# A decoder layer in split fp32 on one core: lo parts written over loaded tiles, and shorter pauses before the up projection

## The chip, the cores and the metric

The kernel runs on one core of a Trainium2 chip. The metric is the device time of one execution in microseconds. A core has TensorE (PE in the profile: matmuls and transposes), VectorE (DVE), ScalarE (ACT), GpSimd (POOL, nearly unused here) and SyncE (SP, which issues the DMA transfers in the order of its queue). "PEld" is the loading of weights into TensorE.

## The reference

One layer of a decoder over 2048 positions of 1024 channels, all in float32:

```python
h = rms_norm(x, mix_norm_g)
z = h @ w_in                                   # 1024 -> 2048
lru_x, lru_gate, conf_a, conf_b = split(z, 4)
y_lru = rg_lru(causal_dwconv(lru_x, ...), ...) * gelu(lru_gate)
c = silu(layer_norm(causal_dwconv(conf_a * sigmoid(conf_b), ...)))
x = x + concat([y_lru, c]) @ w_out

h, m = rms_norm(x, xa_norm_g), rms_norm(mem, mem_norm_g)
q, (k, v) = h @ w_q, split(m @ w_kv, 2)        # 256 memory tokens, 4 heads
p = softmax(q @ k.T * XA_HD ** -0.5)
x = x + (p @ v) @ w_o

h = rms_norm(x, ffn_norm_g)
g, u = split(h @ w_up, 2)                      # 1024 -> 2 x 3072
g = causal_dwconv(g, ffn_conv_w, ffn_conv_b)
x = x + (gelu(g) * u) @ w_down                 # 3072 -> 1024
return rms_norm(x, final_norm_g)
```

## The kernel before

**Split products.** A float32 matrix is split in two parts that TensorE multiplies at its rounded fp32 rate: `hi`, the value rounded (written by ScalarE as a copy), and `lo`, the value less `hi` (a subtraction by VectorE). A product of two such matrices is three matmuls, hi x hi, lo x hi and hi x lo (`mm3`). In the names of the profile `yh`/`yl`, `Xh`/`Xl`, `wh`/`wl` and `hidh`/`hidl` are such pairs. `parts(b)` makes the pair of a tile `b` in two new tiles; `split(src, hi, lo)` does it into tiles that were made before by `pair`.

**Seven products.** The large matrix products are done as 2 x 2 blocks with seven block products in place of eight, with sums and differences of blocks as operands (named S1 to S4 on one side and T1 to T4 on the other). `Quads` prepares the seven operands of three weight matrices ahead of time and keeps their pairs in DRAM: OUT_Q (w_out), A_Q (queries against memory keys), VO_Q (memory values times w_o; `VO` in the profile's DMA rows). `seven` runs the seven products of a stage of `attend(h)`, FIRST (w_out), SECOND (scores) and THIRD (probabilities times VO), for half `h` of the positions. In THIRD the last three products are P7, P2 and P3; `x_...` in the rows below are the residual tiles to which VectorE adds their banks, and `yh`/`yl` with `s<-pt,s` are the split of their left operand.

**The up projection.** `up(h, B)` goes over half `h` in blocks of columns; each block is seven products (`strassen_cols`) with weights loaded and split on the way (`raw`, `s`, `t`, `wh`, `wl`) and with operands `X` that are made once for a half (`HalfX.make`: loads `xn`, makes the differences `t`, and splits each into `Xh`, `Xl`). For half 0, `make` is called for the first four operands by a task `first_x` while the attention of half 1 still runs, with a pause between them; the three others are made by the first block itself. For half 1 the differences are made ahead by `X[1].kept` and come back as tiles `tx`; all seven operands of half 1 are made during the last block of half 0. `feed_forward` starts when both `first_x` and the last attention step are through. `T:xn`, that is `ps<-ident,xn` in the rows, are the transposes of normed tiles.

**The down projection.** `prepare_down` makes the seven operands of w_down and keeps their pairs in DRAM, paced along the up projection; `Down` loads hidden tiles, adds, splits and multiplies them.

**What sets the order.** The kernel is not written in the order in which it runs. Tasks (Python generators) record operations into a `Program`; `drive` advances the task that is due, by a clock of the matmuls recorded so far, and `yield n` asks to be called again n us later on that clock. When all is recorded, `schedule` gives each engine its own list: it simulates the engines with estimated lengths, picks the ready operation with the earliest due time, and gives tiles of a fixed set to those who ask, in the order in which they were recorded. The set has 85 slots of 128 x 512 floats, and 8 banks of PSUM. Every instruction bears the same line number, that of the place where lists are written out, so instructions are told apart by the names of their tiles.

Of the kernel before, what the change touches and what calls it, by code (L numbers as in the profile page):

```python
# [17 lines left out]
P = 128  # L18
# [81 lines left out]
class Ref:  # L100
    def __init__(self, buf, steps, dummy):
        self.buf, self.steps, self.dummy = buf, steps, dummy

    def __getitem__(self, i):
        return Ref(self.buf, self.steps + (lambda ap: ap[i],), self.dummy[i])

    def f32(self):
        return Ref(self.buf, self.steps + (lambda ap: ap.bitcast(F32),), self.dummy)
# [22 lines left out]
def resolve(a):  # L131
    return a.resolve() if isinstance(a, Ref) else a

# [13 lines left out]
class Program:  # L147
# [51 lines left out]
    def do(self, eng, name, out, *args, reads=(), writes=(), **kw):  # L199
        outs = [out] + ([kw["accum_out"]] if "accum_out" in kw else [])  # L200
        ins = [a for a in list(args) + list(kw.values()) if isinstance(a, Ref) and a not in outs]
        if eng == "PE":
            o = self.group or self.op("PE")
            n = ins[1].n if name == "matmul" else P
            if name == "matmul":
                rounded = ins[1].buf.dtype == F32R
                cost = (n + 32) / 2400.0 if rounded else n * 4 / 2400.0
            else:
                cost = 0.11
# [11 lines left out]
        o.calls.append((name, (out,) + args, kw))  # L221
        self.touch(
# [225 lines left out]
def hybrid_layer(  # L448
# [629 lines left out]
    class Quads:  # L1078
# [7 lines left out]
        def prepare(self, pace):  # L1086
            sub = ALU.subtract
            for i in range(KH):
# [37 lines left out]

    held = [0]

    def seven(order, L, W, add, amid):
        banks, left = {}, {}  # L1130
# [4 lines left out]
        for n, (p, bank, start, outs) in enumerate(order):  # L1135
# [4 lines left out]
            for i in range(KH):  # L1140
                lh, ll = parts(L.get(akey, i))
# [246 lines left out]
    class HalfX:  # L1388
# [40 lines left out]
        def make(self, key):  # L1429
            sub = ALU.subtract  # L1430
            if key in self.t:
# [13 lines left out]
            for b in src:  # L1445
                hi, lo = pair("X")
                split(b[:], hi, lo)
                self.B[key].append((hi, lo))

    def strassen_cols(c0, B, outs, used=None):  # L1450
# [11 lines left out]
        def product(bank, src, key, start):  # L1462
            X = B.get(key)
            wh, wl = pair("w", (P, KQ, P))
            split(src, wh, wl)
# [25 lines left out]
        product(c, s1[:], "T1", True)  # L1491
        yield 0
        s3 = comb(a11, a21, ALU.subtract)
        product(a, s3[:], "T3", False)
# [8 lines left out]
        product(c, s4[:], "B22", False)  # L1503
# [54 lines left out]
    def prepare_down():  # L1558
        yield attends[NH - 1]
        for c in range(NCK):  # L1560
            for i in range(KD):
                f = c * 2 * KD + i
                raw = []
                for r0 in (f * P, (f + KD) * P):
                    for half in range(2):
                        t = tmp("wd")
                        pr.dma(t[:], w_down[0, r0 : r0 + P, half * TT : (half + 1) * TT])
                        raw.append(t[:])
                b11, b12, b21, b22 = raw
                t1 = combine("t", b12, b11, ALU.subtract)  # L1570
                t2 = combine("t", b22, t1[:], ALU.subtract)
                t3 = combine("t", b22, b12, ALU.subtract)
                t4 = combine("t", b21, t2[:], ALU.subtract)
                for key, src in (("B11", b11), ("B21", b21), ("T2", t2[:]), ("T1", t1[:]), ("T3", t3[:]), ("T4", t4[:]), ("B22", b22)):
                    hi, lo = pair("w")
                    split(src, hi, lo)
# [5 lines left out]
    class Down:  # L1582
# [34 lines left out]
        def gather(self, c, n):  # L1617
# [192 lines left out]
```

## Time and profile before

| | us |
|---|---|
| median of 3 runs | 2493.47 |
| lowest and highest run | 2490.45, 2495.44 |
| the profiled execution | 2495.1 |
| its span, first to last instruction | 2493.3 |
| TensorE busy | 2421.8 |
| VectorE busy | 1921.3 |
| ScalarE busy | 1290.6 |

The mean granted clock of TensorE in the profiled execution is 0.988 of full speed. The times of a span are counted from its start. A row of a timeline gives the start, the length, the engine, the operation with the tiles it writes and reads, its size and the number of like instructions, and in brackets the idle time of the engine before it with what ended it. A row of the view by stages gives, for each engine, the busy time and the number of instructions, then the granted clock, the busy share of the DMA engines, and GB/s.

### The profile page before, as it was taken

Reading aid. Unit: us, or ns where it says so; the run is one execution under the profiler, and the core shown is the slowest. Engines: PE = TensorE matmul, PEld = TensorE weight load, DVE = VectorE, ACT = ScalarE, POOL = GpSimd, SP = SyncE. Lnnn points to the kernel's source line nnn. Section 1 sums busy time; section 2 is a strip of 40 time slices with the busy share of each in tenths; the row PEclk is TensorE's granted clock in tenths of the full one; section 3 lists DMA queues with packets and bytes.
Section 4 is the critical chain, followed back from the end, with each engine's and each line's share of the span. In section 5 each row is a group of like instructions: output and inputs, shape, how many; then the busy total and the mean of one; then the engine's idle time right before and its main releaser. Section 6 shows DMA issues by size and latency. Waiting matters only on the chain.

```text
span 2493.3 us, 32519 instructions
## 1 busy us (share of the span) xinstructions
PE 2421.8 (97%) x10788; PEld 1988.5 (80%) x10788; DVE 1921.3 (77%) x3187; ACT 1290.6 (52%) x2256; POOL 0.7 (0%) x6
## 2 busy tenths in 40 slices
PE   6999999999998999999999999999999999999998
PEld 5788868877767888878888887788888888888886
DVE  4579968999988645779888887987876775667665
ACT  8426668266977655775545455654443431233222
POOL 0000000000000000000000000000000000000000
PEclk8999999999999999999999999999999999999999
DMA  6987678797786966586654546644422288769774
GB/s 221 376 296 228 228 237 302 248 349 243 241 300 224 372 221 228 167 278 241 226 204 155 182 162 194 235 166 163 169 76 85 93 293 269 249 224 368 257 251 157
DMA packets 339839, 572.07 MB, mean 229 GB/s; under 512 B 32925, under 2 KB 106653, under 8 KB 339671
## 3 DMA queue, kind: packets, MB, share of 16 engines
q1 hardware_dynamic: 339670, 570.00, 67.0%
q8 instruction: 85, 1.39, 0.2%
q14 instruction: 84, 0.68, 0.1%
HBM read 385.32 MB, written 184.55 MB: 229 GB/s over the span
## 4 chain that ended last, share of the span: by engine, by line
PE 87%; DVE 5%; DMA 4%; ACT 3%; issue 1%; SPq 0%; DVEq 0%; ACTq 0%
PE ps L420 87%; ACT prob L420 1%; DVE yl L420 1%; DMA raw<-in_w_out_dram 1%; DVE t L420 1%; DMA VO<-VO 0%; DMA x<-in_x_dram 0%; DMA yf<-yf 0%; DVE s L420 0%; DVE prob L420 0%; DVE xc L420 0%; DVE gate L420 0%; ACT L420 0%; DVE Xl L420 0%; ACT x L420 0%
## 5 line engine op out<-in xcount | busy, mean ns | idle before, releaser
L420 PE MATMUL ps<-Xh,wl 128*128 128x512 f32 x1344 | 523.9, 390 | 2.5 <-DVE wl L420 2.5
L420 PE MATMUL ps<-Xh,wh 128*128 128x512 f32 x1344 | 524.3, 390 | 1.6 <-ACT wh L420 1.6
L420 PE MATMUL ps<-Xl,wh 128*128 128x512 f32 x1344 | 523.4, 389 | 0.0
L420 PEld LDWEIGHTS ps<-Xh,wl 128*128 128x128 f32 x1344 | 252.6, 188 | 57.1 <-DVE wl L420 4.7
L420 PEld LDWEIGHTS ps<-Xh,wh 128*128 128x128 f32 x1344 | 252.7, 188 | 55.3 <-ACT wh L420 2.9
L420 PEld LDWEIGHTS ps<-Xl,wh 128*128 128x128 f32 x1344 | 252.7, 188 | 52.1
L420 PE MATMUL ps<-wh,yh 128*128 128x512 f32 x672 | 268.9, 400 | 7.0 <-ACT pt L420 3.7
L420 PE MATMUL ps<-wh,yl 128*128 128x512 f32 x672 | 265.0, 394 | 4.9 <-DVE yl L420 4.9
L420 PE MATMUL ps<-wl,yh 128*128 128x512 f32 x672 | 264.5, 394 | 0.1
L420 PE MATMUL ps<-wh,hidh 128*128 128x512 f32 x672 | 261.4, 389 | 0.0
L420 PE MATMUL ps<-wl,hidh 128*128 128x512 f32 x672 | 261.4, 389 | 0.0
L420 PE MATMUL ps<-wh,hidl 128*128 128x512 f32 x672 | 261.4, 389 | 0.0
L420 DVE TENSOR_TENSOR acc<-acc,ps 128x512 f32<-128x512 f32 x192 | 129.5, 685 | 150.3 <-PE ps L420 149.9
L420 PE MATMUL ps<-xh,wh 128*128 128x512 f32 x512 | 201.8, 394 | 0.9 <-DMA wh<-w_in 0.8
L420 PE MATMUL ps<-xh,wl 128*128 128x512 f32 x512 | 199.5, 390 | 2.3 <-DVE wl L420 1.7
L420 PE MATMUL ps<-xl,wh 128*128 128x512 f32 x512 | 199.3, 389 | 0.0
L420 ACT ACTIVATE wh<-s 128x512 fp32r<-128x512 f32 x192 | 119.8, 629 | 136.5 <-DVE s L420 99.9
L420 PEld LDWEIGHTS ps<-wh,yh 128*128 128x128 f32 x672 | 128.0, 191 | 36.9 <-ACT pt L420 4.6
L420 PEld LDWEIGHTS ps<-wh,yl 128*128 128x128 f32 x672 | 127.9, 190 | 34.1 <-DVE yl L420 7.1
L420 DVE TENSOR_TENSOR wl<-s,wh 128x512 fp32r<-128x512 f32 x192 | 131.2, 688 | 27.3 <-ACT wh L420 25.4
L420 ACT ACTIVATE u<-ps 128x512 f32<-128x512 f32 x144 | 85.9, 597 | 126.5 <-PE ps L420 125.4
L420 PEld LDWEIGHTS ps<-wl,yh 128*128 128x128 f32 x672 | 128.2, 191 | 27.6 <-issue 0.8
(200 smaller groups left out, 4113.0 us busy)
## 6 DMA issues: line engine op xcount, KB each, us to landing
raw<-in_w_up_dram SPq DMA_DIRECT2D x96, 512.0 KB
wh<-w_down SPq DMA_DIRECT2D x164, 256.0 KB
wl<-w_down SPq DMA_DIRECT2D x164, 256.0 KB
hid<-cv SPq DMA_DIRECT2D x48, 512.0 KB
h<-hid SPq DMA_DIRECT2D x96, 256.0 KB
w_down<-wh SPq DMA_DIRECT2D x84, 256.0 KB
w_down<-wl SPq DMA_DIRECT2D x84, 256.0 KB
x<-in_x_dram SPq DMA_DIRECT2D x64, 256.0 KB
```

Of the source, the lines that this page charges most:

```text
L420: getattr(e, name)(*[resolve(a) for a in args], **{k: resolve(a) for k, a in kw.items()})
```

## The change

Two things are changed. First, `split_over(b)` makes the pair of a tile whose last use is this split: `hi` goes into a new tile, and `lo` is written over `b` itself, if `b` was loaded by DMA and no engine has written it since; else `lo` gets a new tile as before. It stands in `Quads.prepare`, in `seven` for the last use of a block, in `HalfX.make` (for all operands of half 1, and for the differences and the last block of half 0), in `strassen_cols`, in `prepare_down` and in `Down.gather`. The test on loaded tiles leaves 116 tiles: 36 in `Quads.prepare` (b11, b21, b22 of four steps of three matrices), 4 (the last block) of half 0's operands, all 28 of half 1's, 36 in `prepare_down`, and 12 in `Down` (A22 of half 0). The sums and differences that VectorE makes in the kernel get a new tile for `lo` as before. Second, `first_x` pauses 5 us on the recorder's clock after each of its four operands, where it paused 20. No operation is added or taken away.

```diff
@@ class Buf
-        self.ops, self.heads = [], []
+        self.ops, self.heads, self.loaded = [], [], True
@@ class Ref
+    def r(self):
+        return Ref(self.buf, self.steps + (lambda ap: ap.bitcast(F32R),), self.dummy, True)
...
+class Over:
+    def __init__(self, buf):
+        self.buf, self.dtype = buf, F32R
+
+    def __getitem__(self, i):
+        return self.buf[i].r()
@@ Program.do
+        for r in outs:
+            if not r.rounded:
+                r.buf.loaded = False
@@
+    def split_over(b, name):
+        hi, lo = rnd(name + "h", b.shape), Over(b) if b.loaded else rnd(name + "l", b.shape)
+        ACT(hi[:], b[:], AF.Copy)
+        V("tensor_tensor", lo[:], b[:], hi[:].f32(), op=ALU.subtract)
+        return hi, lo
@@ Quads.prepare
-                    for j, b in enumerate(parts(t)):
+                    for j, b in enumerate(split_over(t, "y")):
@@ seven
-                lh, ll = parts(L.get(akey, i))
+                lh, ll = split_over(L.get(akey, i), "y") if n in spent else parts(L.get(akey, i))
@@ HalfX.make
             for b in src:
-                hi, lo = pair("X")
-                split(b[:], hi, lo)
+                if self.h or key[0] == "T" or key == "B22":
+                    hi, lo = split_over(b, "X")
+                else:
+                    hi, lo = pair("X")
+                    split(b[:], hi, lo)
@@ prepare_down
-                    hi, lo = pair("w")
-                    split(src, hi, lo)
+                    hi, lo = split_over(src, "w")
@@ Down.gather
-                hi, lo = pair("hid")
-                split(src[:], hi, lo)
+                if akey in ("S1", "S3", "S4") or (akey == "A22" and not self.h):
+                    hi, lo = split_over(src, "hid")
+                else:
+                    hi, lo = pair("hid")
+                    split(src[:], hi, lo)
@@ first_x
         for key in UP_ORDER[:EARLY]:
             X[0].make(key)
-            yield 20
+            yield 5
```

Both move instructions, since the schedule is worked out anew from the tiles asked for and the order of recording. Three places are shown, each before and after.

TensorE, the end of the attention of half 1. The rows are the last products of THIRD (`wh`, `wl` are VO's pairs), the transposes of normed tiles, and the first products of the up projection (`Xh`, `Xl`). Before:

```order
L420 MATMUL ps<-wh,yh 128x512
L420 MATMUL ps<-wl,yh 128x512
L420 MATMUL ps<-wh,yl 128x512
L420 MATMUL ps<-ident,xn 128x128 x16
L420 MATMUL ps<-Xh,wh 128x512
L420 MATMUL ps<-Xl,wh 128x512
L420 MATMUL ps<-Xh,wl 128x512
L420 MATMUL ps<-Xh,wh 128x512
```

Changed:

```order
L436 MATMUL ps<-wh,yh 128x512
L436 MATMUL ps<-wl,yh 128x512
L436 MATMUL ps<-wh,yl 128x512
L436 MATMUL ps<-Xh,wh 128x512
L436 MATMUL ps<-Xl,wh 128x512
L436 MATMUL ps<-Xh,wl 128x512
L436 MATMUL ps<-Xh,wh 128x512
L436 MATMUL ps<-Xl,wh 128x512
```

In the changed order 144 up matmuls (six products) follow directly; then eight transposes stand, and the others in groups between later products.

VectorE, during P2 and P3 of the same stage. `x_...` are residual adds of P7 and P2 (the tile numbers differ between the kernels), `t<-xn` starts and `t<-xn,t` continues the differences for `X`, `yl<-s,yh` splits P3's operand. Before:

```order
L420 TENSOR_TENSOR x_7923<-x_7923,ps 128x512
L420 TENSOR_TENSOR x_7925<-x_7925,ps 128x512
L420 TENSOR_TENSOR t<-xn 128x512
L420 TENSOR_TENSOR x_7927<-x_7927,ps 128x512
L420 TENSOR_TENSOR x_7931<-x_7931,ps 128x512
L420 TENSOR_TENSOR t<-xn 128x512 x3
L420 TENSOR_TENSOR t<-xn,t 128x512 x6
L420 TENSOR_TENSOR x_8186<-x_8186,ps 128x512
L420 TENSOR_TENSOR t<-xn,t 128x512
L420 TENSOR_TENSOR Xl<-t,Xh 128x512
```

Changed:

```order
L436 TENSOR_TENSOR x_7887<-x_7887,ps 128x512
L436 TENSOR_TENSOR t<-xn 128x512 x2
L436 TENSOR_TENSOR yl<-s,yh 128x512
L436 TENSOR_TENSOR t<-xn,t 128x512
L436 TENSOR_TENSOR x_7889<-x_7889,ps 128x512
L436 TENSOR_TENSOR t<-xn,t 128x512 x2
L436 TENSOR_TENSOR s<-pt,s 128x512
L436 TENSOR_TENSOR t<-xn,t 128x512
L436 TENSOR_TENSOR x_7895<-x_7895,ps 128x512
L436 TENSOR_TENSOR yl<-s,yh 128x512
L436 TENSOR_TENSOR Xl<-t,Xh 128x512 x2
```

The differences for `X` have moved ahead of P2's adds and among the splits of P3's operand, which stood before them.

VectorE, the last block of half 0 of the up projection. `gb` and `up` take a bank out of PSUM, `cv` is the convolution over 1024 positions, `s` the weights' sums, `wl` their lo parts, `Xl` (in the changed kernel `xn`, the loaded tile itself) the lo parts of half 1's operands. Before:

```order
L420 TENSOR_TENSOR gb<-u,ps 128x512
L420 TENSOR_TENSOR Xl<-xn,Xh 128x512
L420 COPY gtail<-gb 128x2
L420 SCALAR_TENSOR_TENSOR cv<-gb,v_110,cv 128x1024
L420 TENSOR_TENSOR s<-raw 128x512
L420 TENSOR_TENSOR wl<-t,wh 128x512
L420 TENSOR_TENSOR s<-s,raw 128x512
L420 TENSOR_TENSOR up<-u,ps 128x512
L420 SCALAR_TENSOR_TENSOR cv<-gb,v_110,cv 128x1024
L420 TENSOR_TENSOR wl<-s,wh 128x512 x2
```

Changed:

```order
L436 TENSOR_TENSOR xn<-xn,Xh 128x512 x3
L436 TENSOR_TENSOR s<-raw 128x512
L436 TENSOR_TENSOR gb<-u,ps 128x512
L436 COPY gtail<-gb 128x2
L436 TENSOR_TENSOR s<-s,raw 128x512
L436 SCALAR_TENSOR_TENSOR cv<-gb,v_110,cv 128x1024
L436 TENSOR_TENSOR wl<-s,wh 128x512
L436 SCALAR_TENSOR_TENSOR cv<-gb,v_110,cv 128x1024
L436 TENSOR_TENSOR up<-u,ps 128x512
L436 TENSOR_TENSOR wl<-t,wh 128x512
L436 TENSOR_TENSOR wl<-s,wh 128x512
```

The first `wl<-s,wh` has moved ahead of the second convolution step, of `up` and of the `wl<-t,wh` that stood before it.

More of the change, by code (lines that the diff above doesn't have):

```diff
@@ L100, with __init__ @@
 class Ref:
[L101 removed]
+    def __init__(self, buf, steps, dummy, rounded=None):
         self.buf, self.steps, self.dummy = buf, steps, dummy
+        self.rounded = buf.dtype == F32R if rounded is None else rounded
     def __getitem__(self, i):
[L105 removed]
+        return Ref(self.buf, self.steps + (lambda ap: ap[i],), self.dummy[i], self.rounded)
     def f32(self):
[L108 removed]
+        return Ref(self.buf, self.steps + (lambda ap: ap.bitcast(F32),), self.dummy, False)
+    def r(self):
+        return Ref(self.buf, self.steps + (lambda ap: ap.bitcast(F32R),), self.dummy, True)
     def split2(self, k):
@@ L205, in do @@
             if name == "matmul":
-                rounded = ins[1].buf.dtype == F32R
-                cost = (n + 32) / 2400.0 if rounded else n * 4 / 2400.0
+                cost = (n + 32) / 2400.0 if ins[1].rounded else n * 4 / 2400.0
             else:
@@ L1125, in hybrid_layer, with last_uses, make @@
              ("P7", "a", False, [C21, C22]), ("P2", "a", True, [C11]), ("P3", "b", False, [C12]))
+    NEEDS = dict(S1=("A21", "A22"), S2=("S1", "A11"), S3=("A11", "A21"), S4=("A12", "S2"))
+    def last_uses(keys):
+        made, uses = set(), {}
+        def make(key, n):
+            if key in NEEDS and key not in made:
+                made.add(key)
+                for k in NEEDS[key]:
+                    make(k, n)
+                    uses[k] = n
+        for n, key in enumerate(keys):
+            make(key, n)
+        return [n for n, key in enumerate(keys) if uses.get(key, -1) <= n]
     held = [0]
     def seven(order, L, W, add, amid):
+        spent = last_uses([PRODUCTS[p][0] for p, _, _, _ in order])
         banks, left = {}, {}
@@ L1430, in make @@
             sub = ALU.subtract
+            assert not self.h or self.t or key[0] == "B"
             if key in self.t:
@@ L1460, in comb, with product @@
             return t
-        def product(bank, src, key, start):
+        def product(bank, src, key, start, over=None):
             X = B.get(key)
-            wh, wl = pair("w", (P, KQ, P))
-            split(src, wh, wl)
+            if over:
+                wh, wl = split_over(over, "w")
+            else:
+                wh, wl = pair("w", (P, KQ, P))
+                split(src, wh, wl)
             with together():
@@ L1490, in strassen_cols @@
         c = ps()
-        product(c, s1[:], "T1", True)
+        product(c, None, "T1", True, s1)
         yield 0
         s3 = comb(a11, a21, ALU.subtract)
-        product(a, s3[:], "T3", False)
+        product(a, None, "T3", False, s3)
         u3 = copied(a)
@@ L1502, in strassen_cols @@
         s4 = comb(a12, s2[:], ALU.subtract)
-        product(c, s4[:], "B22", False)
+        product(c, None, "B22", False, s4)
         outs(0, 1, u2, c)
@@ L1567, in prepare_down @@
                         pr.dma(t[:], w_down[0, r0 : r0 + P, half * TT : (half + 1) * TT])
-                        raw.append(t[:])
+                        raw.append(t)
                 b11, b12, b21, b22 = raw
[L1570 to L1574, printed above, removed]
-                    hi, lo = pair("w")
-                    split(src, hi, lo)
+                t1 = combine("t", b12[:], b11[:], ALU.subtract)
+                t2 = combine("t", b22[:], t1[:], ALU.subtract)
+                t3 = combine("t", b22[:], b12[:], ALU.subtract)
+                t4 = combine("t", b21[:], t2[:], ALU.subtract)
+                for key, src in (("B11", b11), ("B21", b21), ("T2", t2), ("T1", t1), ("T3", t3), ("T4", t4), ("B22", b22)):
+                    hi, lo = split_over(src, "w")
                     at = wd_at(c, key, i)
```

1 line of the change is left out of this document (added).

## The prediction, as it was put on record before the result

> **What bounds the kernel now.** I read the page first, then the busy time by stage, then the timelines of TensorE, VectorE and ScalarE around the stages that are not full. The page's span, its first row of engines and its chain of waits:
>
> ```profile
> span 2493.3 us, 32519 instructions
> PE 2421.8 (97%) x10788; PEld 1988.5 (80%) x10788; DVE 1921.3 (77%) x3187; ACT 1290.6 (52%) x2256; POOL 0.7 (0%) x6
> PE 87%; DVE 5%; DMA 4%; ACT 3%; issue 1%; SPq 0%; DVEq 0%; ACTq 0%
> ```
>
> TensorE is busy 97% of the span and 87% of the chain that ended last. The change takes no matmul away, so it can only win or lose in the 71 us in which TensorE stands, and where its clock is low. Stage by stage (busy time and count of each engine, then granted clock, DMA share, GB/s):
>
> ```profile
> core 0: us, PE busy (x) PEld busy (x) DVE busy (x) ACT busy (x) POOL busy (x), PEclk, DMA share, GB/s
> 0.00:60.00 60.00, 38.61 (x186) 32.59 (x187) 23.81 (x113) 48.73 (x107) 0.70 (x6) 0.89 0.67 219
> 60.00:545.00 485.00, 481.19 (x2141) 389.56 (x2140) 407.91 (x658) 276.61 (x437) 0.00 (x0) 1.00 0.82 282
> 545.00:700.00 155.00, 144.66 (x638) 115.60 (x637) 149.17 (x261) 114.38 (x203) 0.00 (x0) 0.96 0.75 247
> 700.00:800.00 100.00, 88.70 (x378) 69.92 (x377) 95.36 (x169) 76.64 (x159) 0.00 (x0) 0.93 0.77 267
> 800.00:1087.00 287.00, 283.25 (x1338) 236.40 (x1337) 172.39 (x310) 169.20 (x377) 0.00 (x0) 0.99 0.74 254
> 1087.00:1123.00 36.00, 29.75 (x147) 24.36 (x146) 25.70 (x44) 32.44 (x62) 0.00 (x0) 0.86 0.74 251
> 1123.00:1545.00 422.00, 422.00 (x1863) 349.31 (x1862) 359.90 (x573) 214.75 (x328) 0.00 (x0) 1.00 0.56 192
> 1545.00:1570.00 25.00, 21.31 (x86) 15.42 (x86) 23.95 (x37) 20.46 (x35) 0.00 (x0) 1.00 0.83 276
> 1570.00:2483.00 913.00, 912.31 (x4025) 755.32 (x4023) 657.29 (x1021) 336.32 (x553) 0.00 (x0) 1.00 0.59 203
> 2483.00:2493.30 10.30, 0.00 (x0) 0.00 (x0) 5.77 (x11) 1.02 (x3) 0.00 (x0) 0.68 0.57 212
> ```
>
> From 1123 to 1545 TensorE is never idle: 1863 matmuls in 422 us, 0.2265 us each, which I call dense. Six stages have holes: the first 60 us and the last 10.3 us, which the new order leaves as they were; 545 to 800 (mixing and attention of half 0, with VectorE busy 149.17 of 155.00 us and then 95.36 of 100.00); 1087 to 1123 (start of the up projection); 1545 to 1570 (half 0 to half 1 of the up projection). The change moves work at the last three.
>
> **Part A, the up projection's start (1087 to 1123).** TensorE's timeline (start, length, operation, and in brackets the idle time before it and what ended it) and the clock:
>
> ```profile
> 1076.87 0.39 PE L420 MATMUL ps<-wh,yh 128*128 128x512 f32 x1
> 1087.52 0.39 PE L420 MATMUL ps<-wh,yl 128*128 128x512 f32 x1
> 1093.34 4.88 PE L420 MATMUL ps<-ident,xn 128*128 128x128 f32 x16 [5.43 <-ACT xn L420]
> 1097.87 0.78 PE L420 MATMUL ps<-Xh,wh 128*128 128x512 f32 x1
> 1100.92 0.39 PE L420 MATMUL ps<-Xl,wh 128*128 128x512 f32 x1
> 1111.17 2.79 PE L420 MATMUL ps<-ident,xn 128*128 128x128 f32 x24
> 1113.71 0.48 PE L420 MATMUL ps<-Xh,wh 128*128 128x512 f32 x1
> 1093.30:1098.00 4.70, 4.25 (x17) 3.37 (x17) 2.19 (x5) 4.70 (x9) 0.00 (x0) 0.50 1.01 387
> 1098.00:1101.00 3.00, 3.00 (x10) 2.37 (x9) 3.00 (x6) 2.31 (x5) 0.00 (x0) 0.53 0.80 253
> ```
>
> The last attention product ends about 1087.9, and the 16 transposes of the last normed tiles wait 5.43 us for ScalarE's `xn`. Behind this wait the clock stands at 0.50: the 16 transposes take 4.53 us up to the next matmul at 1097.87, where 24 later ones take 2.54 (1111.17 to 1113.71), which for 16 makes 1.69, so 2.84 is lost; seven matmuls fill 1097.87 to 1100.92, 3.05 us where dense ones take 7 x 0.2265 = 1.58, so 1.47 more. Together 5.43 + 2.84 + 1.47 = 9.74.
>
> The shorter pauses put 144 up matmuls (32.6 us dense) straight behind the attention's last product, and the transposes behind those: the three losses go. In exchange the operands `Xl` and the lo weights must be made earlier, by VectorE, among the attention's last residual adds. How fast VectorE gets through there, and where it stands:
>
> ```profile
> 1064.15 4.87 DVE L420 TENSOR_TENSOR x<-x,ps 128x512 f32<-128x512 f32 x8 [3.00 <-PE ps L420]
> 1072.61 0.16 DVE L420 TENSOR_TENSOR small<-small 128x4 f32<-128x4 f32 x1 [1.18 <-ACT junk L420]
> 1074.22 0.18 DVE L420 RECIPROCAL small<-small 128x4 f32<-128x4 f32 x1 [1.45 <-ACT small L420]
> 1075.71 1.37 DVE L420 TENSOR_TENSOR x<-x,ps 128x512 f32<-128x512 f32 x2 [1.31 <-PE ps L420]
> 1097.90 0.69 DVE L420 TENSOR_TENSOR s<-raw 128x512 f32<-128x512 f32 x1 [2.50 <-PE ps L420]
> ```
>
> Eight adds in 4.87 us: about 0.60 each. I count the changed order's VectorE instructions from 1064.15, the first of those adds, at 0.60 each and with 0.76 for one wait on TensorE (the add at 1075.71). The attention's last product P3 starts at 1076.87 and takes 12 x 0.2265 = 2.72 for each of its four steps. Its third `yl` is the 30th instruction: ready at 1082.9, wanted at 1082.75, 0.3 late with the margin of a restart; its fourth, the 36th: 1086.6 against 1085.75, 0.9 late. The up products then run from about 1089.4, 2.72 each. The lo weights of T3 (58th, 1099.8) and T4 (64th, 1103.4) come in time; that of B22, the 71st, at 1107.6 against 1106.2, is 1.4 late. With 0.27 lost at each of three restarts (a matmul after a wait below takes 0.50 where it takes 0.39) that is 0.3 + 0.9 + 1.4 + 0.8 = 3.4. **Term A: 3.4 - 9.7 = -6.3**, between -9.7 (nothing late) and 0 and beyond (below, the slower rival).
>
> TensorE: Matmul & The Clock Gate in the Trainium skill, section "HAM oscillation", says no idle gap of TensorE should exceed some 3.4 us, since its clock is halved then; the trace agrees (0.50 behind 5.43 us idle), and by that rule waits of 0.3 to 1.4 us cost only themselves.
>
> **Part B, half 0 to half 1 (1545 to 1570).** 86 matmuls stand where 25.00 / 0.2265 = 110.4 fit, not counting wait by wait: the stage holds 5.5 us of hole (24.4 matmuls). What TensorE waits for, with ScalarE's and VectorE's rows:
>
> ```profile
> 1543.65 0.69 DVE L420 TENSOR_TENSOR gb<-u,ps 128x512 f32<-128x512 f32 x1
> 1548.41 1.15 ACT L420 ACTIVATE wh<-s 128x512 fp32r<-128x512 f32 x2 [1.44 <-PE ps L420]
> 1549.62 0.50 PE L420 MATMUL ps<-Xh,wh 128*128 128x512 f32 x1 [0.56 <-ACT wh L420]
> 1550.96 1.29 DVE L420 TENSOR_TENSOR wl<-s,wh 128x512 fp32r<-128x512 f32 x2
> 1551.70 0.50 PE L420 MATMUL ps<-Xh,wl 128*128 128x512 f32 x1 [1.35 <-DVE wl L420]
> ```
>
> The waits are for weights split just in time, `wh` held up until TensorE gives a tile free, `wl` standing behind an `Xl` of half 1, the gates' convolution and other weights. In the changed kernel the 28 lo parts of half 1 go over their loaded tiles, so 28 grants of a tile fall away, and in VectorE's order `wl<-s,wh` follows the last `gb` of that block after three instructions (one of them 1024 wide) where it followed after eight (two of them wide). The trace has 7.31 us from that `gb` to `wl` (1543.65 to 1550.96); counting a wide one double that is 7.31 / 11 = 0.66 for each unit with the `gb` itself, so 5 x 0.66 = 3.3 us in the new order, 4.0 earlier, where the longest wait for `wl` was 1.35. I take the larger part, four fifths of 5.5: **term B: -4.5**, between -5.5 and 0 (the stage stays).
>
> Writing in place costs the subtraction itself nothing, by the nearest rows (busy time and mean ns of one, then idle time before):
>
> ```profile
> L420 DVE TENSOR_TENSOR gate<-gate,m 128x512 f32<-128x512 f32 x16 | 11.0, 685 | 3.0 <-ACT m L420 3.0
> L420 DVE TENSOR_TENSOR wl<-raw,wh 128x512 fp32r<-128x512 f32 x176 | 119.2, 688 | 29.8 <-ACT wh L420 24.3 <-PE ps L420 4.8
> ```
>
> 685 ns over its own operand, 688 ns into a new tile. Of 116 such tiles, 36 in the three weights prepared for out and attention, 36 in the down weights and 12 in the down product lie in stages whose TensorE is full (60 to 545, 1123 to 1545, 1570 to 2483): hidden behind matmuls, worth nothing; uncovered, each would cost or save 0 to 3 ns. A loaded tile is held longer now (till its last matmul), and one slot less is asked for: no slot more at any time.
>
> **Part C, mixing and attention of half 0 (545 to 800).** The freed slots shift the schedule slightly: some `gate` groups come 12 matmuls later, one group of transposed probabilities 6 matmuls earlier, and ScalarE's order holds 81 table loads instead of 75.
>
> ```profile
> L420 ACT ACT_TABLE_LOAD x75 | 96.2, 1283 | 2.4 <-PEq L1796 0.7 <-DVE gate L420 0.4
> 641.99 1.28 ACT L420 ACT_TABLE_LOAD   x1
> 643.28 1.27 ACT L420 ACTIVATE gate<-ps,v 128x512 f32<-128x512 f32 x2
> 757.57 2.73 PE L420 MATMUL ps<-ident,prob 128*128 128x128 f32 x9 [5.32 <-ACT prob L420]
> ```
>
> Six more loads are 6 x 1.283 = 7.7 us of ScalarE if all are passed on, through a VectorE that is full here. ScalarE is idle for 155 - 114.38 = 40.6 and 100 - 76.64 = 23.4 us in these stages, so most vanish. The six matmuls (1.36 us) now stand behind the probabilities instead of filling the wait of 5.32 us: I take **+1.0**, between -3 (two table loads and a later group of probabilities saved) and +8.
>
> ScalarE: Activation LUTs in the Trainium skill, section "What ACT_TABLE_LOAD costs", adds a drain of 1.38 us to each load of 1.28, 2.66 in all; by it the six would be up to 16 us (an estimate from that page). Here the next ACTIVATE starts at 643.28, right at the load's end, and all 75 loads had 2.4 us of idle time before them: no drain is seen, so the row decides.
>
> **Sum.** -6.3 - 4.5 + 1.0 = -9.8 us. The profiled execution took 2495.1 us, 2493.3 of span and 1.8 around it; so 2483.5 of span, 2485.3 executed. The runs' median, 2493.47, is 1.6 below the profiled one: 2493.47 - 9.8 = 2483.7, forecast **2484**.
>
> **The rivals.** (1) *One hole stays or is handed on.* If VectorE is late all along P3 and eats term A, -4.5 + 1.0 = -3.5: 2490.0; for it speaks that VectorE idles between 1064 and 1098 for things it cannot hurry, against it that the 71 instructions fit but for 1.4 us. If term B stays, -5.3: 2488.2; for it, that ACT `wh` waits for TensorE itself (1.44). If the table loads are passed on whole, -9.8 - 1.0 + 7.7 = -3.1: 2490.4; for it, the full VectorE, against it, ScalarE's 64 us of idle time.
>
> (2) *Nothing is late*, -9.7 - 5.5 = -15.2: 2478.3; for it, that VectorE's rows at 1075.71 include idle time that other work may fill.
>
> (3) *Slower: VectorE is the new bound at the start.* Its row of instructions still holds waits: 3.00 + 1.18 + 1.45 + 1.31 + 2.50 = 9.44 us above. In the new order `t<-xn`, which needs loads from SP's queue, stands on VectorE among P3's `yl`, and on SP's queue P3's last two weight pairs stand behind a store that waits for VectorE's own add. If all 9.4 is passed on to TensorE in two waits long enough to drop the clock, each with the 2.84 + 1.47 = 4.3 seen behind the 5.43: -9.8 + 9.4 + 8.6 = +8.2: 2501.7. It decides once VectorE idles by more than some 9 us in all, or one wait lies clearly above the 1.35 us behind which the clock stayed at 1.00 and near the 5.43 us behind which it was 0.50. Against it: the waits at 1072.61 and 1074.22 are for norms that now stand behind the adds.
>
> (4) *A table load costs ScalarE twice its row*, for an emptying of the engine that the row doesn't show: the six, wholly passed on, put 2 x 7.7 = 15.4 in the place of 1.0: +4.6, 2498.1. Against it, the 643.28 right behind 641.99 + 1.28. (It is what Activation LUTs in the Trainium skill would have.)
>
> **Chances.** The forecast .48; rival 2 .09; rival 1 .30 (A .12, B .08, loads .10); rival 3 .11; rival 4 .02. About 5 us (0.2%) is what a measurement can tell from no change: below 2488.5 lie the forecast, rival 2 and part of B's case, .62; within 5 us the rest of rival 1, .25; above, .13. The likeliest case's own range is 2479 to 2488. For 8 in 10 I reach over rival 1 and half way into 3 and 4: 2476 to 2497.
>
> **What would show it.** A right: no wait for `xn` after the last attention product, the clock at 1.00 from 1087 to 1105, waits for `yl` and `wl` of 2 to 4 us together. B right: 1545 to 1570, moved with the earlier stages, holds over 105 matmuls. C right: the time up to the first attention's end moves by less than 2 us. Wrong, if TensorE waits more than 3 us at once for `yl`, `s` or VO's weights before the up projection, if a wait for a tile takes the place of that for `wl`, or if 545 to 800 grows by more than 4 us.

## The result, and the profile after

The changed kernel takes 2485.89 us (median of six runs, 2483.22 to 2486.93) where the kernel before takes 2494.11 (six runs, 2490.45 to 2495.44): a ratio of 0.9964, with a 95% interval of 0.9952 to 0.9977. That is 8.2 us less; forecast were 9.8 less and 2484. The profiled execution took 2486.16 us, with 2484.4 of span.

The page of the changed kernel, its span, engines and chain of waits:

```profile
span 2484.4 us, 32511 instructions
PE 2418.1 (97%) x10788; PEld 1985.5 (80%) x10788; DVE 1916.4 (77%) x3187; ACT 1294.7 (52%) x2262; POOL 0.7 (0%) x6
PE 68%; DVE 9%; ACT 2%; DMA 2%; issue 1%; SPq 0%; DVEq 0%; ACTq 0%
```

ScalarE has six instructions more (2262 for 2256), the six table loads. Three of the stages with holes, as a view of the changed kernel (columns as in the prediction):

```profile
545.00:700.00 155.00, 141.30 (x628) 112.33 (x627) 150.63 (x260) 112.06 (x198) 0.00 (x0) 0.98 0.76 250
1087.00:1123.00 36.00, 34.26 (x149) 27.37 (x149) 35.10 (x61) 26.56 (x51) 0.00 (x0) 1.00 0.48 154
1545.00:1570.00 25.00, 24.36 (x107) 19.35 (x106) 25.00 (x41) 22.93 (x42) 0.00 (x0) 1.00 0.85 300
```

At the start of the up projection TensorE is busy 34.26 of 36.00 us (before 29.75) and its clock is 1.00 (before 0.86), while VectorE is now busy 35.10 (before 25.70): TensorE's hole is gone, and with it nearly all of VectorE's idle time there. At the passage from half 0 to half 1 there are 107 matmuls in 25 us, where there were 86 (106 when the window is set 5.18 us earlier, by which the changed kernel is ahead there). What TensorE still waits for from the attention's last products to the second block of half 1, from its timeline:

```profile
1088.66 0.50 PE L436 MATMUL ps<-wh,yl 128*128 128x512 f32 x1 [0.29 <-DVE yl L436]
1091.04 0.39 PE L436 MATMUL ps<-Xh,wh 128*128 128x512 f32 x1
1105.50 0.50 PE L436 MATMUL ps<-Xh,wl 128*128 128x512 f32 x1 [0.25 <-DVE wl L436]
1109.71 0.50 PE L436 MATMUL ps<-Xh,wl 128*128 128x512 f32 x1 [1.20 <-DVE wl L436]
1550.22 0.50 PE L436 MATMUL ps<-Xh,wl 128*128 128x512 f32 x1 [0.45 <-DVE wl L436]
1555.73 0.47 PE L436 MATMUL ps<-Xh,wh 128*128 128x512 f32 x1 [0.19 <-DVE up L436]
1575.49 0.50 PE L436 MATMUL ps<-Xh,wh 128*128 128x512 f32 x1 [0.38 <-DVE gb L436]
```

No wait for `xn` is left, and every wait is 1.20 us or shorter. (The 144 up matmuls that now follow the last attention product are twelve products of 12 matmuls, not six as the words under the order rows have it; the prediction's 2.72 us a product is for 12.)

To compare stages in all kernels I take marks in TensorE's timeline that each of them has: the start of the last transposes of probabilities in the attention, and of the 401st, the 641st and the last product `Xh,wl`. Before and changed:

```profile
1039.75 1.91 PE L420 MATMUL ps<-ident,prob 128*128 128x128 f32 x16
2027.68 0.39 PE L420 MATMUL ps<-Xh,wl 128*128 128x512 f32 x1
```

```profile
1042.41 1.91 PE L436 MATMUL ps<-ident,prob 128*128 128x128 f32 x16
2018.76 0.39 PE L436 MATMUL ps<-Xh,wl 128*128 128x512 f32 x1
```

The 401st starts at 1377.99 before and 1372.81 changed, the 641st at 1541.19 and 1536.01. So the *start* (probabilities to 401st) takes 338.24 and 330.40 us, -7.84; 401st to 641st 163.20 in both; the *passage* (641st to last) 486.49 and 482.75, -3.74. The changed kernel reaches the mark of the probabilities 2.66 later. Behind the last one, up to the end of the span, it takes 465.64 for 465.62. In sum 2.66 - 7.84 - 3.74 = -8.92, the difference of the two spans (8.9).

### The profile page after: what moved, and what is told of

Read it like the earlier page. It is cut to its first block, busy times and chain, and to the rows that moved or that the text cites. A ratio compares the mean times of both kernels' runs of the same rounds, so it can differ in the third digit from the quotient of the medians.

```text
span 2484.4 us, 32511 instructions
## 1 busy us (share of the span) xinstructions
PE 2418.1 (97%) x10788; PEld 1985.5 (80%) x10788; DVE 1916.4 (77%) x3187; ACT 1294.7 (52%) x2262; POOL 0.7 (0%) x6
## 4 chain that ended last, share of the span: by engine, by line
PE 68%; DVE 9%; ACT 2%; DMA 2%; issue 1%; SPq 0%; DVEq 0%; ACTq 0%
PE ps L436 68%; ACT prob L436 1%; DVE e L436 1%; DVE f L436 1%; DVE yl L436 1%; DVE so L436 1%; DVE s L436 1%; DVE t L436 0%; DVE x L436 0%; DVE gate L436 0%; DVE Xl L436 0%; DVE conv L436 0%; DVE prob L436 0%; DVE xc L436 0%; DMA wh<-w_out 0%
## 5 line engine op out<-in xcount | busy, mean ns | idle before, releaser
L436 PE MATMUL ps<-wh,hidl 128*128 128x512 f32 x624 | 242.7, 389 | 0.0
L436 PE MATMUL ps<-Xl,wh 128*128 128x512 f32 x576 | 224.1, 389 | 0.0
L436 ACT ACTIVATE hidh<-s 128x512 fp32r<-128x512 f32 x96 | 58.9, 631 | 176.2 <-DVE s L436 140.9
L436 ACT ACTIVATE wh<-raw 128x512 fp32r<-128x512 f32 x176 | 107.8, 626 | 80.2 <-PE ps L436 58.9
```

The source lines that it names most:

```text
L436: getattr(e, name)(*[resolve(a) for a in args], **{k: resolve(a) for k, a in kw.items()})
```

## The experiments

The table is the key to all of them: the ratio to the kernel before, and the two stages in the profiled execution, in us. A gain or loss of the whole time, in the text below, is a kernel's median less that of the kernel before in the same comparison.

| kernel | ratio, 95% interval | start | passage |
|---|---|---|---|
| before | 1 | 338.24 | 486.49 |
| changed | 0.9964 (0.9952 to 0.9977) | 330.40 | 482.75 |
| pause_alone | 0.9986 (0.9977 to 0.9994) | 332.60 | 486.76 |
| over_alone | 0.9991 (0.9982 to 1.0000) | 338.23 | 482.26 |
| half1_alone | 0.9984 (0.9975 to 0.9992) | 336.83 | 482.26 |
| quads_alone | 1.0004 (0.9995 to 1.0012) | 338.29 | 486.48 |
| over_without_quads | 0.9956 (0.9943 to 0.9970) | 330.40 | 482.75 |
| over_without_half1 | 0.9988 (0.9980 to 0.9997) | 330.42 | 488.68 |
| pause_10 | 0.9969 (0.9958 to 0.9981) | 333.08 | 480.76 |
| double_lo | 0.9984 (0.9975 to 0.9993) | 335.97 | 482.75 |
| pause_and_b22 | 0.9978 (0.9968 to 0.9988) | 330.40 | 488.33 |
| pause_10_without_quads | 0.9960 (0.9948 to 0.9973) | 333.04 | 480.76 |
| seven_early | 0.9958 (0.9945 to 0.9970) | 331.27 | 482.00 |

Kernels with the same order in a stage agree there within 0.1 us unless the clock differed (338.24 and 336.83; so too 486.76 and 488.33, with the same waits in slightly different orders), as told below. What lies ahead of the mark of the probabilities moves from execution to execution by up to 6 us: it takes 1037.56 to 1043.57 in the eight traces that have TensorE's order of the kernel before there.

### The pause alone

```diff
         for key in UP_ORDER[:EARLY]:
             X[0].make(key)
-            yield 20
+            yield 5
```

> The kernel before with pauses of 5 for 20, nothing written over loaded tiles (75 table loads as before). Theory, each part has its own cause (the pause gives the start of the up projection, the overwritten tiles of half 1 give the passage from half 0 to half 1, the overwritten tiles of the weight preparation cost something in the mixing stage): the two traces have +2.6 us up to the last probabilities, -7.8 over the start and -3.7 over the passage, so here -8 of the kernel before, ratio 0.9968, no wait for xn after the last attention product, and the passage at 1545 as before (some 86 matmuls in its 25 us, waits for wh and wl). Rival 1, the early operands need the slots that overwriting sets free: less than half, -4 or nothing, with new waits for tiles at the start. Rival 2, the pause alone moves the passage too: -11 to -12.

Measured: 0.9986, -3.3 us, not -8. The wait for `xn` is gone and the passage is as before, as expected. But the start holds 332.60 us, 2.20 more than in the changed kernel. TensorE's timeline there:

```profile
1105.46 0.67 PE L420 MATMUL ps<-Xh,wl 128*128 128x512 f32 x1 [1.80 <-DVE wl L420]
1105.93 0.63 PE L420 MATMUL ps<-Xh,wh 128*128 128x512 f32 x1
...
1108.91 0.46 PE L420 MATMUL ps<-Xl,wh 128*128 128x512 f32 x1
1109.21 0.40 PE L420 MATMUL ps<-Xh,wl 128*128 128x512 f32 x1
```

The wait for the seventh product's `wl` is 1.80 us where the changed kernel has 1.20, and behind it matmuls stand 0.43 us apart, not 0.23: eight of them from 1105.46 to 1108.91 take 3.45 where dense ones take 1.81, 1.6 us lost. My theory that each part has its own cause falls for this part. So does rival 1 as it was put: its size, less than half, came out, but no wait for a tile appears. VectorE's rows tell what is ahead of that `wl`, first in the pause alone, then in the changed kernel:

```profile
1099.91 0.68 DVE L420 TENSOR_TENSOR wl<-raw,wh 128x512 fp32r<-128x512 f32 x1
1100.52 0.68 DVE L420 TENSOR_TENSOR gb<-u,ps 128x512 f32<-128x512 f32 x1
1101.11 0.69 DVE L420 TENSOR_TENSOR s<-raw,s 128x512 f32<-128x512 f32 x1
1101.72 0.68 DVE L420 TENSOR_TENSOR gb<-u,ps 128x512 f32<-128x512 f32 x1
1102.31 2.49 DVE L420 TENSOR_TENSOR Xl<-xn,Xh 128x512 fp32r<-128x512 f32 x4
1104.72 0.68 DVE L420 TENSOR_TENSOR wl<-s,wh 128x512 fp32r<-128x512 f32 x1
```

```profile
1104.76 0.68 DVE L436 TENSOR_TENSOR wl<-raw,wh 128x512 fp32r<-128x512 f32 x1
1105.37 0.69 DVE L436 TENSOR_TENSOR s<-raw,s 128x512 f32<-128x512 f32 x1
1105.97 0.68 DVE L436 TENSOR_TENSOR xn<-xn,Xh 128x512 fp32r<-128x512 f32 x1
1106.57 0.68 DVE L436 TENSOR_TENSOR gb<-u,ps 128x512 f32<-128x512 f32 x1
1107.17 1.89 DVE L436 TENSOR_TENSOR xn<-xn,Xh 128x512 fp32r<-128x512 f32 x3
1108.97 0.69 DVE L436 TENSOR_TENSOR wl<-s,wh 128x512 fp32r<-128x512 f32 x1
```

Two `gb` stand ahead of it in the one, one in the other: 0.60 us, the difference of the waits. The lo parts of B22 are the four tiles of half 0 that the change writes over. That is the new theory, tried by pause_and_b22 below.

### Overwriting alone

> The changed kernel with the pauses of 20 kept: lo parts over loaded tiles alone (81 table loads). Theory: the wait of about 5.4 us for xn and the low clock behind it are there as before, the passage is shorter by 3.7, the stage of mixing and first attention longer by 2.6: -1.1, ratio 0.9996. Rival 1, overwriting alone frees enough for the start as well: -5 or more. Rival 2, the 2.6 is scatter of one execution: -3.7.

The edit is the changed kernel with `yield 20` kept. Measured: 0.9991, -2.3 us. The start is as before (338.23; the wait for `xn` is 5.43), so rival 1 falls; the passage is 4.23 shorter. The theory's -1.1 and rival 2's -3.7 both lie inside the interval.

### The operands of half 1 alone

```diff
-                if self.h or key[0] == "T" or key == "B22":
+                if self.h:
                     hi, lo = split_over(b, "X")
```

with `yield 20`, and `split` into new tiles in the preparations and in `Down`.

> Overwriting only for the seven operands of half 1 of the up projection, 28 tiles, pauses of 20 (75 table loads). Theory: only the passage moves, from 86 matmuls in its 25 us to about 105, and the time by -3.7, ratio 0.9985. Rival, the passage was shortened in the changed kernel by something else (the up blocks that stand elsewhere after the early start, or the overwritten down weights): no change, 0 to -1, and the waits for wh and wl as before.

Measured: 0.9984, -4.6 us (forecast 0.9985, -3.7). The passage is 482.26, 4.23 shorter than before, with one wait of 0.41 us left of six. These 28 tiles make the passage; the rival falls. Whether it is the grants saved or the place of single instructions in the new order isn't separated. Its start differs from that of the kernel before by 1.41 with the same wait for `xn`: the clock behind that wait came back earlier (it is 0.50 for 6.83 us from 1094.94, before for 10.24 us from 1090.55).

### The weight preparation alone

```diff
-                if self.h or key[0] == "T" or key == "B22":
+                if False:
```

with `yield 20`, `split` in `prepare_down` and `Down`, and only `Quads.prepare` writing over its tiles.

> Overwriting only in the preparation of the three weight matrices of out and attention, 36 tiles, pauses of 20. ScalarE's order here has 81 table loads, where it has 75 before. Theory: these tiles are what costs in the stage of mixing and first attention: +2.6, ratio 1.0010, with the probabilities of 757.57 about 3 us later, and nothing else moved. Rival 1, the loads are hidden and the 2.6 is scatter: 0, 1.0000. Rival 2, each load passed on: +7.7, 1.0031.

Measured: 1.0004, +0.9 us, with 81 table loads as in the changed kernel. All loads passed on (1.0031) is excluded; between +2.6 and nothing this run doesn't decide. The view by groups shows for this kernel that the loads take 1283 ns each as before, with hardly any idle time ahead of them:

```profile
L436 ACT ACT_TABLE_LOAD x81 | 103.9, 1283 | 3.7 <-DVE gate L436 1.2 <-PEq L1845 0.7 <-PE ps L436 0.4
```

### All but the weight preparation

```diff
-                    for j, b in enumerate(split_over(t, "y")):
+                    for j, b in enumerate(parts(t)):
```

> The changed kernel, but without overwriting in the preparation of the three weight matrices (75 table loads): pauses of 5, and overwriting in the up and down projections. Theory: those 36 tiles cost about 1 us in the stage of mixing and first attention (they alone measured +0.9) and give nothing elsewhere, so this is -9 of the kernel before, ratio 0.9963, about 1 below the changed kernel. Rival 1, the freed slots of the preparation are what makes the early start good in the changed kernel (the pause alone gave -3.2 where the start of the changed kernel holds -8): then the start is here as in the pause alone, with a wait for wl of about 1.8 and the low clock behind it, and the time about -3.2 - 4.6 = -7.5, 0.9970. Rival 2, nothing there matters: as the changed kernel, 0.9967.

Measured: 0.9956, 2483.54 us, -10.7, with 75 table loads. Start and passage are to the hundredth those of the changed kernel, so rival 1 falls, and what it gains over the changed kernel (2.4 us) lies ahead of the probabilities' mark. The intervals of the two kernels overlap.

### All but half 1

```diff
-                if self.h or key[0] == "T" or key == "B22":
+                if not self.h and (key[0] == "T" or key == "B22"):
```

> The changed kernel, but the operands of half 1 of the up projection in new tiles. Theory: the passage from half 0 to half 1 is as before (waits for wh and wl, 5.5 us of hole), so the changed kernel's -8.2 loses the 4.6 that half 1 alone gave: -3.6, ratio 0.9986. Rival, the overwritten tiles of the down weights ease the passage too: -6 to -8.

Measured: 0.9988, -3.4 us (forecast -3.6). The start is the changed kernel's. The passage is 2.19 us longer than before, some 1.6 of it by a lowered clock; so without these tiles nothing is won there. Its two longest waits, the second with the clock lowered:

```profile
1557.38 0.50 PE L436 MATMUL ps<-Xh,wh 128*128 128x512 f32 x1 [2.30 <-ACT wh L436]
1559.13 0.60 PE L436 MATMUL ps<-Xh,wl 128*128 128x512 f32 x1 [1.01 <-DVE wl L436]
```

### Pauses of 10

```diff
-            yield 5
+            yield 10
```

> The changed kernel with pauses of 10 for 5. TensorE's order has 48 up matmuls (10.9 us) ahead of the first transposes of normed tiles, where the changed kernel has 144 and the kernel before none. Theory, the wait of 5.43 us for xn is all that has to be covered, and whatever covers it does: no wait for xn, no low clock, and VectorE has more room; -8 to -10, ratio 0.9965. Rival 1, VectorE is the limit of this stage and later transposes only help it: waits for xn or for lo parts of 2 us and more come back, with the clock lowered behind them: -4 or less, ratio 0.9984 or above.

Measured: 0.9969, -8.3 us by the medians of that comparison, as the changed kernel. The theory's size came out, its reason only in part: the start is 2.68 longer than with 5, because a short wait for `xn` is left after 48 up matmuls and the transposes come one by one behind it, and the passage is 1.99 shorter, which I had not expected:

```profile
1099.66 0.33 PE L436 MATMUL ps<-ident,xn 128*128 128x128 f32 x1 [1.05 <-ACT xn L436]
1100.27 0.33 PE L436 MATMUL ps<-ident,xn 128*128 128x128 f32 x1 [0.28 <-ACT xn L436]
1104.10 0.50 PE L436 MATMUL ps<-Xh,wh 128*128 128x512 f32 x1 [0.96 <-ACT wh L436]
```

So 10.9 us of other work doesn't quite cover the chain behind the attention's last product, and 32.6 us does.

### The lo parts of two operands written twice

```diff
                     hi, lo = split_over(b, "X")
+                    if not self.h and key in ("T2", "T1"):
+                        V("tensor_tensor", lo[:], b[:], hi[:].f32(), op=ALU.subtract)
```

Eight VectorE instructions of some 0.60 us are added.

> The changed kernel with the lo parts of T2 and T1 of half 0 written twice: 8 more VectorE instructions of about 0.60 us, 4.8 us in all, between the attention's last products and the first up products. Theory, VectorE has no idle time left there (its rows follow one another without a gap from 1066 to 1100) and TensorE is just not kept waiting (0.29, 0.25 and 1.20 us): the 4.8 is passed on to TensorE, and where one wait passes about 1.8 the clock drops for some eight matmuls (1.6 us): 5 to 8 us above the changed kernel, ratio to the kernel before 0.9987 to 1.0000. Rival, VectorE's row is filled with work that isn't wanted yet and has slack: less than 1.5 above the changed kernel, 0.9967 to 0.9973.

Measured: 0.9984, by the medians 4.4 us above the changed kernel, just below the theory's 5 to 8, and 5.57 in the start (335.97 for 330.40), inside it. With 1.6 of the 5.57 for the low clock, some 4.0 of the 4.8 us of work were passed on. TensorE waited 0.35, 0.46, 0.41 and 0.17 us for `yl`, `yh` and `Xl`, and then:

```profile
1103.10 0.63 PE L436 MATMUL ps<-Xh,wl 128*128 128x512 f32 x1 [1.91 <-DVE wl L436]
1103.53 0.63 PE L436 MATMUL ps<-Xh,wh 128*128 128x512 f32 x1
...
1111.66 0.50 PE L436 MATMUL ps<-Xh,wl 128*128 128x512 f32 x1 [1.23 <-DVE wl L436]
```

Again eight matmuls at 0.43 us behind a wait of nearly 2. VectorE is the engine that sets the pace of the start now.

### The pause and one operand

The edit is the pause of 5, and `split_over` for B22 of half 0 only (`if not self.h and key == "B22"`).

> Pauses of 5, and overwriting for one operand only: the four tiles of B22 of half 0 (75 table loads). In the pause alone one more bank add (gb) stands on VectorE ahead of the lo part of B22's weights; TensorE waited 1.80 us for it and its next eight matmuls took 0.425 us each. In VectorE's order here that add stands behind, as in the changed kernel. Theory, this one instruction is the difference between the two starts: a wait of 1.2 and full clock behind it, and 2.05 us less than the pause alone: -5.4 of the kernel before, ratio 0.9978. Rival, the starts differ by scatter or by tiles set free elsewhere: as the pause alone, a wait of 1.8 with low clock behind it, 0.9986.

Measured: 0.9978, as the theory had it, and 1.5 us below the pause alone. The intervals of the two ratios overlap a little, but the start decides: 330.40, the changed kernel's to the hundredth, with waits of 0.23 and 1.20 and no low clock:

```profile
1102.79 0.50 PE L436 MATMUL ps<-Xh,wl 128*128 128x512 f32 x1 [0.23 <-DVE wl L436]
1107.01 0.50 PE L436 MATMUL ps<-Xh,wl 128*128 128x512 f32 x1 [1.20 <-DVE wl L436]
```

One instruction of 0.60 us, standing ahead or behind, made 2.20 us of the start: 0.6 as wait, 1.6 as lowered clock. Up to that `wl` VectorE's row holds the same instructions but for this one bank add. Why the schedule moves it when B22 is written over, no run shows.

### The pause alone, once more

> The kernel of the pause alone once more. Its profiled execution took 2487.5, the lowest of eleven, where most took 2490.3. Theory, a wait of the same length lowers the clock in some executions and not in others (behind the probabilities near 763 the first matmul took 0.50 us in that execution and 0.79 in that of the kernel before, after waits of 1.14 and 1.08): in an execution of about 2490.3 the clock is low there or behind another wait of 1 to 3 us, for some 2 us in all, and the waits themselves are the same. Rival, an execution of 2490.3 has another wait, for VO's weights (0.48 in the first profile), of 2 us and more.

The same kernel as pause_alone. This execution took 2490.62 us, 3.1 more than the first one profiled. Its start (332.58) and passage (486.74) are the first one's, with the wait for `wl` 1.79 and the low clock again. All 3.1 lie ahead of the probabilities' mark (1040.70 for 1037.56), and 2.15 of it already ahead of the first attention product (540.46 for 538.31). The rival misses: there is no wait for VO's weights of 2 us. The theory looked in the wrong place, for the matmul behind the probabilities near 763 took 0.50 in both, but it has the cause of most of the 3.1. In both executions TensorE waits twice for weights of w_in near 502, 0.84 and 0.94 us in the first and 0.93 and 0.77 in this one, and only in this one the clock is lowered behind them. TensorE's busy time, count and clock (then DMA share and GB/s), first in the first execution, then in this one:

```profile
501.48:504.89 3.41, 2.44 (x9) 1.00 1.05 401
```

```profile
501.30:504.71 3.41, 1.71 (x7) 1.00 1.05 398
504.71:508.12 3.41, 3.41 (x10) 0.50 1.03 390
```

Ahead of this place this execution lies 0.71 us behind the first, after it 2.22. It has made up 1.2 of that by 580, and from 680 to 700, with the clock at 0.50 for 10.24 us in two stretches (in the first execution for 3.41), it falls from 1.0 to 3.1 behind, where it stays.

So a single profile can't price what lies in the first 1040 us to better than some 3 us, and here the clock made most of the difference.

### Two combinations

Pauses of 10 without the weight preparation:

> Pauses of 10, overwriting in the up and down projections only (75 table loads). Theory, the parts add: without the 36 tiles of the weight preparation -10.7 was measured with pauses of 5; with pauses of 10 the start was 2.7 us longer and the passage 2.0 shorter, so -10: ratio 0.9960, as fast as the pauses of 5 without those tiles. Rival, the passage gets shorter by itself with 10 and the start's extra was scatter: -12, 0.9952.

Measured: 0.9960, 2483.16 us, start and passage as with pauses of 10; the parts add.

All seven operands of half 0 recorded early (`EARLY = 7`), pauses of 5, without the weight preparation:

> As the changed kernel without overwriting in the weight preparation, but all seven operands of half 0 recorded early (four before), pauses of 5. On VectorE the loads' differences for T3 and the lo parts of B22's operand stand earlier, bank adds later; on TensorE 96 up matmuls stand ahead of the first transposes, where 144 stood. Theory, VectorE has idle time before 1066 (4.91 and 2.69 us in the changed kernel) but not behind it, and recording earlier moves little into it: the start has about the same waits of 1.2 to 2 us, -10 to -11, ratio 0.9958. Rival 1, the work moves into the idle time, all waits vanish: -12.5, 0.9950. Rival 2, P3's own operand is pushed back by it: waits for yl of over 2 us with the clock lowered, -6, 0.9976.

Measured: 0.9958, 2482.68 us. The start is 331.27, with four waits of 0.16 to 0.78 us where there were three, and the passage 482.00. The time is the theory's forecast, while the waits are shorter than its 1.2 to 2 us; neither rival is seen. These two and over_without_quads gain 2.1 to 2.6 us more than the changed kernel and can't be told from one another.

## Why the prediction was right

Direction, time and the likeliest case held: 2485.89 lies in the range and in the likeliest case's own (2479 to 2488). That the sum came so near is in part luck: in the two spans term A was off by -1.5 us, B by +0.8 and C by +1.7, which cancel to +0.9. Of its signs, the wait for `xn` is gone, the clock is 1.00, and 1545 to 1570 holds over 105 matmuls; the waits at the start, 1.74 us together, are less than the 2 to 4 foreseen, and the sign for C missed, as told under it. By its steps:

**Term A, -6.3; measured -7.84.** The removal was as worked out: the wait for `xn` is gone and the clock is 1.00. The new waits were put at 0.3, 0.9 and 1.4 us, for P3's third and fourth `yl` and B22's `wl`, 2.6 in all; measured are 0.29 (the fourth `yl`), 0.25 (T4's `wl`, said to be in time) and 1.20 (B22's): 1.74. With 0.27 for each of three restarts that is 2.55, so -9.74 + 2.55 = -7.2; the rest is the kernel before's own wait of 0.41 for a `wl` at 1122.11 and its restart, which went too and which I hadn't counted:

```profile
1122.11 0.50 PE L420 MATMUL ps<-Xh,wl 128*128 128x512 f32 x1 [0.41 <-DVE wl L420]
```

Counting VectorE's instructions at 0.60 each from one known start held over 71 of them to a few tenths of a microsecond (from 1066.81, the first of the eight adds, to 1109.66, the end of B22's `wl`: 42.85 for 71 x 0.60 = 42.6). What was off is the 0.76 us put in for a wait on TensorE: VectorE's row has no gap there, so P3's splits came earlier than foreseen. That VectorE would be nearly the bound was right: double_lo passed on some 4.0 of its 4.8. What the prediction did not see is that a part of this term hangs on overwriting: it gave the whole to the pause. The pause alone gave 5.64 of it in the start, and the four tiles of B22 the remaining 2.20.

**Term B, -4.5; measured -3.74.** The cause is right: half 1's 28 tiles alone made the passage 4.23 shorter, and without them it was no shorter than before. The size is a little high because 0.45, 0.19 and 0.38 us of wait stayed, with three restarts of 0.27 some 1.8, where 1.0 was left over; 5.5 - 1.8 = 3.7.

**Term C, +1.0; between 0.9 and 2.4, in another place and for another reason.** By medians, the 36 tiles of the weight preparation cost 0.9 when alone, 2.4 when taken from the changed kernel and 2.0 when taken from the one with pauses of 10; no one interval shows that they cost something. The traces show where they do. From 90 to 115 us TensorE falls 3.00 to 3.13 us behind the kernel before in all six traces with these tiles, and at most 0.05 in the seven others without. Two waits of the product with w_in, for a `wh` and a `wl`, are 1.05 and 2.29 us there where they were 0.14 and 1.72, and the clock is 0.50 for 3.41 us behind them (106.83 to 110.25 in the changed kernel). Before, then changed:

```profile
104.99 0.50 PE L420 MATMUL ps<-xh,wl 128*128 128x512 f32 x1 [1.72 <-DVE wl L420]
```

```profile
102.71 0.50 PE L436 MATMUL ps<-xh,wh 128*128 128x512 f32 x1 [1.05 <-ACT wh L436]
105.74 0.50 PE L436 MATMUL ps<-xh,wl 128*128 128x512 f32 x1 [2.29 <-DVE wl L436]
```

None of the six has a table load between 75 and 165 us, so the loads aren't the reason here. Five of the six additional loads run between 340 and 440 us (26 for 21), and there TensorE loses nothing in the changed kernel: it is 1.68 us behind the kernel before at 350 and 1.65 at 470 (the other five lose 0.0 to 0.8 us there). Which tile or instruction lengthened the two waits, no run separates.

So the size of this term was about right and its mechanism wrong. The prediction had looked for a cost of the loads in 545 to 800, and had put the 36 tiles down as worth nothing because TensorE is full from 60 to 545; their new order opened a hole in that full stage. How much of the 3.1 us reaches the end is less sure: the six traces win back 0.5 to 1.3 by 535, and from 535 to 820 they lose 0.1 to 4.2 against the kernel before, where the seven others lie between 1.0 won and 3.1 lost. The sign set for C, less than 2 us up to the first attention's end, missed: the changed kernel is there 2.9 us later in this pair. The chain of the six loads passed on whole (7.7) is excluded.

**The rivals.** A eaten up and B left standing did not happen. The slower rival named the right engine and a wrong condition: a wait near 5.43 us, with 4.3 us of low clock behind it. In this stage waits of 1.79 to 1.91 us were enough in three traces, at a price of 1.6 us. The longest wait of the changed kernel, 1.20, is 0.6 us of VectorE work shorter. The twice-priced table load falls with quads_alone.

By the Trainium skill (ScalarE: Activation LUTs, "What ACT_TABLE_LOAD costs") six loads would be up to 16 us, an estimate of 6 x 2.66; quads_alone, with the six loads, measured +0.9 us and at most 0.12% (3.0).

**Overwriting in place is free**, as was said: the rows `xn<-xn,Xh` above take 0.60 us one after another, like those into new tiles.

## What to carry to other kernels

When a change makes work start earlier, count the instructions on the engine that feeds it, at their spacing in a busy row, from one start that the trace shows; here this gave each new wait to 0.6 us or better, and it tells which single instruction is worth moving. Price a wait on TensorE with what the clock does behind it too: in the two profiled executions here a wait 0.6 us longer cost 2.2. Where two parts of a change land in the same stage, run each alone before giving one of them the whole gain, and leave out a part (here the weight preparation's tiles) that wins in no stage, and look for its cost also in the stages that seem full.

## What the runs showed of the hardware that was not expected

A wait of 1.79 to 1.91 us on TensorE was followed by eight matmuls at 0.43 us each, half speed, in all three executions that had one at this place (both of the pause alone, and double_lo), while waits of 1.20 to 1.23 there were not. But the length alone doesn't decide. In the kernel before a wait of 2.24 us for `gate` was followed by a matmul of 0.80, in the pause alone one of 2.22 at the same place by one of 0.50:

```profile
581.99 0.80 PE L420 MATMUL ps<-wh,yh 128*128 128x512 f32 x1 [2.24 <-ACT gate L420]
```

```profile
580.40 0.50 PE L420 MATMUL ps<-wh,yh 128*128 128x512 f32 x1 [2.22 <-ACT gate L420]
```

The traces' record of the granted clock shows what does. In each of the 14 traces all stretches at 0.50 start on a grid of 3.413 us and last one to three of its steps (3.41, 6.83 or 10.24 us; the last one is cut off by the program's end), and the grid lies differently against the program in each execution. What goes ahead of a drop is idle time of TensorE within one step, by one wait or several. Of the 9854 steps at full clock between 20 and 2470 us, none with less than 1.35 us idle was followed by a step at 0.50, and each with more than 1.92 was; of the 75 in between, 25 were. The 2.24 us of the kernel before lie nearly whole in one step, while the 2.22 of the pause alone are cut by a step's end into 1.80 and 0.42 (TensorE's busy time, count and clock, before and in the pause alone):

```profile
578.56:581.97 3.41, 1.20 (x6) 1.00 0.90 282
581.97:585.38 3.41, 3.39 (x8) 0.50 0.96 323
```

```profile
576.57:579.98 3.41, 1.61 (x8) 1.00 0.93 315
579.98:583.40 3.42, 3.00 (x13) 1.00 0.96 317
```

In the same way over_without_half1 kept full speed right behind 2.30 us, of which 1.42 lie in the step from 1555.96, and lost it when the 1.01 that followed made this 2.43. The pause alone and pause_and_b22 have the same waits in the passage, up to 2.05 us: the one, with at most 1.66 us idle in a step, kept its clock, the other, with 2.39, lost it and took 1.57 us longer. So a wait of some 2 us costs 1.6 us more or not by where the grid happens to lie in an execution and, by the 1.35 above, a wait of 1.2 alone nowhere lowered it in these traces.

TensorE: Matmul & The Clock Gate in the Trainium skill, section "HAM oscillation", puts the limit at idle gaps of some 3.4 us; the runs show the clock lowered behind 1.8 us, so the measurement decides, and gaps well below 3.4 us are not safe in this kernel.
